# Loads and stores of a row gradient: from two DMA queues to one queue in strict turn

## The chip, the cores and the metric

The program runs on one core of a Trainium2 chip and uses no other. The metric is the device time of one execution in microseconds (us), given as the median over runs. Most runs of one kernel agree within 0.3%, so nothing below about half a per cent is read as an effect without several rounds on one chip.

## The reference

```python
def setup_inputs():
    return {"x": np.random.randn(8192, 8192).astype(np.float32)}

def reference(x):
    return np.gradient(x, axis=1)
```

Inside a row each output is half the difference of its two neighbours; at the two ends of a row it is the plain difference. Each element is read once and written once: 268.4 MB in and 268.4 MB out, 512 MiB in all.

## The kernel before

A tile holds two rows for each of the 128 partitions, 64 KB a partition, and there are 32 tiles and 3 buffers. VectorE writes the differences in place (the input sits 64 elements further on in the same buffer), ScalarE halves them. Loads are issued by SyncE on one DMA queue, stores by ScalarE on another.

```python
    R = 2
    SH = 64
    W = R * m
    pool = ctx.enter_context(tc.tile_pool(name="pool", bufs=3))

    # ... diff(b, c0, c1): tensor_sub on VectorE for the interior and for the
    # two end columns of a row, then nc.scalar.mul(..., mul=0.5) on ScalarE

        for i in range(nsets):
            last = i == nsets - 1
            b = pool.tile([P, SH + W], x.dtype)
            ls = m if last else W
            for c0 in range(0, W, ls):
                nc.sync.dma_start(                       # loads: queue of SyncE
                    out=b[:, SH + c0 : SH + c0 + ls],
                    in_=x_sets[i, :, c0 : c0 + ls],
                )
            step = m // 4 if last else m // 2
            for c0 in range(0, W, step):
                diff(b, c0, c0 + step)
                if last:
                    nc.scalar.dma_start(                 # the last tile leaves in 8 pieces
                        out=out_sets[i, :, c0 : c0 + step], in_=b[:, c0 : c0 + step]
                    )
            if not last:
                nc.scalar.dma_start(out=out_sets[i], in_=b[:, 0:W])   # stores: queue of ScalarE
```

Of the kernel before, what the change touches and what calls it, by code (L numbers as in the profile page):

```python
# [1 line left out]

# [4 lines left out]


@with_exitstack
def kernel(  # L10
    ctx: ExitStack,
    tc: tile.TileContext,
    x: bass.AP,
    out: bass.AP,
):





    nc = tc.nc
    P = nc.NUM_PARTITIONS
    n, m = x.shape
    R = 2
    SH = 64
    W = R * m
    nsets = n // (P * R)

    x_sets = x.rearrange("(s p t) m -> s p (t m)", p=P, t=R)
    out_sets = out.rearrange("(s p t) m -> s p (t m)", p=P, t=R)  # L30

    pool = ctx.enter_context(tc.tile_pool(name="pool", bufs=3))

    def diff(b, c0, c1):

        lo, hi = c0, c1
        if c0 % m == 0:
            lo = c0 + 1
            nc.vector.tensor_sub(  # L39
                out=b[:, c0:lo],  # L40
                in0=b[:, SH + c0 + 1 : SH + c0 + 2],
                in1=b[:, SH + c0 : SH + c0 + 1],
            )
        if c1 % m == 0:
            hi = c1 - 1
        nc.vector.tensor_sub(  # L46
            out=b[:, lo:hi],
            in0=b[:, SH + lo + 1 : SH + hi + 1],
            in1=b[:, SH + lo - 1 : SH + hi - 1],
        )  # L50
        if hi < c1:
            nc.vector.tensor_sub(  # L52
                out=b[:, hi:c1],
                in0=b[:, SH + hi : SH + c1],
                in1=b[:, SH + hi - 1 : SH + c1 - 1],
            )
        nc.scalar.mul(out=b[:, lo:hi], in_=b[:, lo:hi], mul=0.5)  # L57

    with tc.manual_schedule():
        for i in range(nsets):  # L60
            last = i == nsets - 1
            b = pool.tile([P, SH + W], x.dtype)

            ls = m if last else W
            for c0 in range(0, W, ls):
                nc.sync.dma_start(  # L66
                    out=b[:, SH + c0 : SH + c0 + ls],
                    in_=x_sets[i, :, c0 : c0 + ls],
                )
            step = m // 4 if last else m // 2  # L70
            for c0 in range(0, W, step):
                diff(b, c0, c0 + step)
                if last:
                    nc.scalar.dma_start(
                        out=out_sets[i, :, c0 : c0 + step], in_=b[:, c0 : c0 + step]
                    )
            if not last:
                nc.scalar.dma_start(out=out_sets[i], in_=b[:, 0:W])


# [1 line left out]
_INS = ['x']  # L82
_OUTS = [((8192, 8192), 'float32')]


# [23 lines left out]
```

## Time and profile before

1249.59 us was the median of three runs (1249.23 to 1252.78); the profiled run had a span of 1246.8 us.

| | before |
|---|---|
| share of the span that the two queues' packets fill, of 16 engines | 49.9% + 49.7% |
| VectorE busy, ScalarE busy | 47%, 37% |
| rate over the span | 431 GB/s |
| one 64 KB packet on one engine, median | 2.418 us |

The page of the profile shows the first three; the packet time is from the trace's packet records, which have the start, length, size and queue of every packet. The row "DMA" is the busy share of the 16 DMA engines in tenths in 40 slices of the span, the row "GB/s" what they moved; "q1" is SyncE's queue, "q10" ScalarE's, with packets, MB and share:

```profile
span 1246.8 us, 665 instructions
DVE 584.6 (47%) x260; ACT 464.9 (37%) x133; POOL 0.2 (0%) x4
...
DMA  9999999999999999999999999999999999999998
GB/s 404 437 435 437 427 421 433 437 437 435 438 435 437 437 435 416 429 437 437 437 433 437 437 435 437 435 414 433 437 437 435 435 438 435 437 435 433 426 426 343
DMA packets 10373, 536.92 MB, mean 431 GB/s; under 512 B 1152, under 2 KB 1152, under 8 KB 1152
...
q1 hardware_dynamic: 4752, 268.44, 49.9%
q10 hardware_dynamic: 5616, 268.44, 49.7%
```

Nine tenths in every slice but the last. The waits of the DMA issuer (who waited for whom, us in total, times, longest; L66 issues the loads):

```profile
SPq L66 <- DMA out_dram<-b: 1127.6, 29, 59.5
...
SPq L66 <- DMA b<-in_x_dram: 20.5, 1, 20.5
```

Loads waited 1,128 us, nine tenths of the span, for the stores that free their buffers. But what waits is the issuer. Whether it costs anything is seen in the engines, and in the middle of the run they had no hole (a hole is time in which none of the 16 engines has a data packet; view by windows: length, busy time of VectorE, ScalarE and GpSimd with counts, TensorE clock, DMA share, GB/s):

```profile
100.00:1150.00 1050.00, 489.59 (x215) 384.81 (x107) 0.00 (x0) 1.00 1.00 434
```

The last view needed is one tile's compute in the timeline, start and length first. The last ScalarE piece of tile 0 begins at 40.86 us, and the store is issued at 44.51, 22 us after the tile landed (22.56):

```profile
22.56 0.16 DVE L39 TENSOR_TENSOR b<-b 128x1 f32<-128x1 f32 x1 [22.56 <-DMA b<-in_x_dram]
...
40.86 3.62 ACT L57 ACTIVATE b<-b 128x4095 f32<-128x4095 f32 x1 [0.84 <-DVE b L46]
...
44.51 0.37 ACTq L78 DMA_DIRECT2D out_dram<-b  x1
```

### The profile page before, as it was taken

What the parts mean: (1) busy time and instruction counts of PE and PEld (TensorE: products, weight loads), DVE (VectorE), ACT (ScalarE), POOL (GpSimd) and SP (SyncE); (2) the same over time, 40 slices, a digit from 0 to 9 for tenths busy, and PEclk for the clock granted to TensorE, in tenths of its full rate; (3) what the DMA queues carried; (4) which work ended last, traced back from release to release, by engine and by line L of the source; (5) the groups of instructions that cost most, each with busy time, mean ns of one, the idle gap of its engine ahead of it and who ended that gap; (6) DMA issues with size and microseconds to landing.
All of it is one profiled execution on the core that took longest, in us unless ns stands there. A gap on an engine that the chain in (4) does not pass through costs nothing.

```text
span 1246.8 us, 665 instructions
## 1 busy us (share of the span) xinstructions
DVE 584.6 (47%) x260; ACT 464.9 (37%) x133; POOL 0.2 (0%) x4
## 2 busy tenths in 40 slices
DVE  2850555335553355533554335553355533555353
ACT  1731443234432344323442234432344323443252
POOL 0000000000000000000000000000000000000000
DMA  9999999999999999999999999999999999999998
GB/s 404 437 435 437 427 421 433 437 437 435 438 435 437 437 435 416 429 437 437 437 433 437 437 435 437 435 414 433 437 437 435 435 438 435 437 435 433 426 426 343
DMA packets 10373, 536.92 MB, mean 431 GB/s; under 512 B 1152, under 2 KB 1152, under 8 KB 1152
## 3 DMA queue, kind: packets, MB, share of 16 engines
q1 hardware_dynamic: 4752, 268.44, 49.9%
q10 hardware_dynamic: 5616, 268.44, 49.7%
q14 instruction: 5, 0.04, 0.0%
HBM read 268.44 MB, written 268.44 MB: 431 GB/s over the span
## 4 chain that ended last, share of the span: by engine, by line
DMA 75%; DVE 16%; another core or an unknown queue 4%; ACT 3%; issue 0%; SPq 0%; DVEq 0%
DMA b<-in_x_dram 38%; DMA out_dram<-b 37%; DVE b L46 16%; ACT b L57 3%; DVE b L39 0%; DVE b L52 0%; SPq L66 0%; DVEq L39 0%
## 5 line engine op out<-in xcount | busy, mean ns | idle before, releaser
L57 ACT ACTIVATE b<-b 128x4095 f32<-128x4095 f32 (+1 forms) x132 | 463.6, 3512 | 747.8 <-DVE b L46 747.8
L46 DVE TENSOR_TENSOR b<-b 128x4095 f32<-128x4095 f32 (+1 forms) x132 | 567.0, 4295 | 4.5
L39 DVE TENSOR_TENSOR b<-b 128x1 f32<-128x1 f32 x64 | 9.9, 155 | 642.3 <-DMA b<-in_x_dram 642.3
L52 DVE TENSOR_TENSOR b<-b 128x1 f32<-128x1 f32 x64 | 10.2, 159 | 2.2
L57 ACT ACT_TABLE_LOAD x1 | 1.3, 1283 | 22.6 <-DMA b<-in_x_dram 22.6
L93 POOL MEMSET const-bfloat16-1.0<- 128x1 bf16 x1 | 0.1, 101 | 0.0
L93 POOL MEMSET const-uint8-127<- 128x1 uint8 x1 | 0.1, 101 | 0.0
L93 POOL MEMSET const-float32-0.0<- 128x1 f32 x1 | 0.1, 98 | 0.2 <-issue 0.2
L93 POOL MEMSET const-float32-1.0<- 128x1 f32 x1 | 0.1, 98 | 0.0
## 6 DMA issues: line engine op xcount, KB each, us to landing
b<-in_x_dram SPq DMA_DIRECT2D x2, 4096.0 KB, 46.8
out_dram<-b ACTq DMA_DIRECT2D x8, 1024.0 KB, 18.7
b<-in_x_dram SPq DMA_DIRECT2D x31, 47.7
out_dram<-b ACTq DMA_DIRECT2D x31, 46.6
```

Source lines behind the costliest of these rows:

```text
L39: nc.vector.tensor_sub(out=b[:, c0:lo], in0=b[:, SH + c0 + 1 : SH + c0 + 2], in1=b[:, SH + c0 : SH + c0 + 1],)
L46: nc.vector.tensor_sub(out=b[:, lo:hi], in0=b[:, SH + lo + 1 : SH + hi + 1], in1=b[:, SH + lo - 1 : SH + hi - 1],)
L52: nc.vector.tensor_sub(out=b[:, hi:c1], in0=b[:, SH + hi : SH + c1], in1=b[:, SH + hi - 1 : SH + c1 - 1],)
L57: nc.scalar.mul(out=b[:, lo:hi], in_=b[:, lo:hi], mul=0.5)
L93: nc = _bacc.Bacc("TRN2", target_bir_lowering=False, num_devices=1)
```

## The change

The intent: with loads and stores on one queue, in strict turn, transfers no longer share the engines; each lands in half the time, and the order is chosen so that one transfer is always queued behind the running one. The load that reuses a buffer (`LAG = 3` buffers) is issued one turn late (`BACK = 1`), behind the next tile's store. So the queue reads load 0, load 1, load 2, store 0, store 1, load 3, store 2, load 4, and so on. The last tile is loaded whole and stored in two pieces.

```diff
-    pool = ctx.enter_context(tc.tile_pool(name="pool", bufs=3))
+    LAG, BACK = 3, 1
+    pool = ctx.enter_context(tc.tile_pool(name="pool", bufs=LAG))
...
+    def load(i):
+        b = pool.tile([P, SH + W], x.dtype)
+        nc.sync.dma_start(out=b[:, SH : SH + W], in_=x_sets[i])
+        return b
...
+        held = [load(i) for i in range(LAG)]
         for i in range(nsets):
-            ... (tile, load, diff, store on nc.scalar)
+            b = held[i]
+            piece = m if i == nsets - 1 else W
+            for c0 in range(0, W, m // 2):
+                diff(b, c0, c0 + m // 2)
+                c1 = c0 + m // 2
+                if c1 % piece == 0:
+                    nc.sync.dma_start(
+                        out=out_sets[i, :, c1 - piece : c1], in_=b[:, c1 - piece : c1]
+                    )
+            j = i - BACK
+            if j >= 0 and j + LAG < nsets:
+                held.append(load(j + LAG))
```

More of the change, by code (lines that the diff above doesn't have):

```diff
@@ L57, in diff @@
         nc.scalar.mul(out=b[:, lo:hi], in_=b[:, lo:hi], mul=0.5)
+    def load(i):
+        b = pool.tile([P, SH + W], x.dtype)
+        nc.sync.dma_start(out=b[:, SH : SH + W], in_=x_sets[i])
+        return b
     with tc.manual_schedule():
+        held = [load(i) for i in range(LAG)]
         for i in range(nsets):
-            last = i == nsets - 1
-            b = pool.tile([P, SH + W], x.dtype)
-            ls = m if last else W
-            for c0 in range(0, W, ls):
-                nc.sync.dma_start(
-                    out=b[:, SH + c0 : SH + c0 + ls],
-                    in_=x_sets[i, :, c0 : c0 + ls],
-                )
-            step = m // 4 if last else m // 2
-            for c0 in range(0, W, step):
-                diff(b, c0, c0 + step)
-                if last:
-                    nc.scalar.dma_start(
-                        out=out_sets[i, :, c0 : c0 + step], in_=b[:, c0 : c0 + step]
-                    )
-            if not last:
-                nc.scalar.dma_start(out=out_sets[i], in_=b[:, 0:W])
+            b = held[i]
[6 more added lines that the diff above has]
+                        out=out_sets[i, :, c1 - piece : c1], in_=b[:, c1 - piece : c1]
+                    )
+            j = i - BACK
+            if j >= 0 and j + LAG < nsets:
+                held.append(load(j + LAG))
 _INS = ['x']
```

## The prediction

> **What bounds it now.** The DMA engines, almost without a break. The page gives the two queues 49.9% + 49.7% of 16 engines' span, VectorE 47%, ScalarE 37%. In the trace's packet records a 64 KB packet takes 2.418 us at the median, load or store: 16 x 65,536 B / 2.418 us = 434 GB/s, against the ceiling of 435 GB/s in the Trainium skill, "DMA: Bandwidth & Descriptors", section "Where 436 GB/s comes from"; this trace agrees. 512 MiB is 512 such packets for each engine: 1238.0 us. The span is 1246.8 us, so under 9 us (0.7%) is anything else:
> - 1.7 us before the first packet of data,
> - 1.7 us of slow first packets (about 3.1 us each), 0.6 us of slow ones later,
> - 0.65 us of completion packets,
> - 0.4 us because the last tile is stored in 8 KB packets (309 ns; eight make 2.47 us),
> - some 3.5 us at the end: engines finishing unevenly, last receipt, last instructions.
>
> From 50 us to the tail, 16 data packets are in flight on average: the two queues leave no gap to fill. The 1,128 us that loads wait for stores (the waits of the DMA queue) are an issuer's waits; the engines are busy with the other queue.
>
> **What the change removes, adds, moves.** Same bytes, same 64 KB packets, same compute. Transfers take turns: each takes about 19.4 us instead of 47. Does the order keep the engines fed? Let load i land at t. Store i-1 runs to t+19.4, load i+1 to t+38.7. A tile's compute takes 22 us (22.56 to 44.51 in the timeline), so store i is queued at t+22, 16 us early; load i+2 waits for store i-1 (t+19.4 and a receipt), is queued just after, and is needed at t+58. At the start loads 0 to 2 run to about 61 us; store 0 is queued at 44.5. At the end store 30 covers most of the last tile's compute. Nothing of compute is exposed.
>
> **Does one queue hand over without a gap?** Loads 0 and 1 landed at about 22.5 and 41.9 us, with one queue running: 19.4 against 8 x 2.418 = 19.34. In the tail, after the last load, stores alone kept 16 packets in flight through four completions. So load to load and store to store cost below 0.1 us. A change of direction on one ring isn't shown by this trace; 63 at 0.1 us would be 6 us.
>
> **Predicted.** Gain: 0.4 us of small packets, perhaps 0.5 us of a tidier end. Loss: 0 to 6 us. I expect 1249.0 us, 8 in 10 between 1246 and 1255. Faster by over 2% would be 1225 us, below the 1238 us of packets. Chances: faster 0.005, same 0.965, slower 0.03.
>
> **What would show it.** One queue with 99% of the span, again 2.418 us a packet; DMA 9 tenths in every slice, some 430 GB/s; each transfer landing about 19.4 us after the one before; tiles computed every 38.7 us; VectorE and ScalarE as busy as before.
>
> **What would make it wrong.** A gap at each change of direction (0.4 us each makes 2%); packets slower when one direction runs alone for long; or load i+2 made to wait for a later store than i-1, which empties the queue for a receipt every turn, seen as deficits in DMA.

## The result and the profile after

| | before | after |
|---|---|---|
| median (range), runs | 1251.16 us (1249.23 to 1252.78), 4 | 1250.30 us (1249.71 to 1250.97), 4 |
| span of the profiled run | 1246.8 us | 1249.0 us |

The ratio is 0.9994, with a 95% interval of 0.9974 to 1.0014: the same.

The page after, with the same rows:

```profile
span 1249.0 us, 619 instructions
DVE 583.8 (47%) x256; ACT 464.1 (37%) x129; POOL 0.2 (0%) x4
...
DMA  9999999999999999999999999999999999999997
GB/s 403 437 432 420 428 432 432 437 434 437 434 424 435 432 434 430 432 437 432 437 434 434 437 434 434 430 428 432 434 428 435 437 430 434 432 437 437 437 437 332
...
q1 hardware_dynamic: 9360, 536.88, 99.6%
```

One queue has replaced two and fills the same 99.6%, and a 64 KB packet again takes 2.418 us at the median. The middle of the run, by windows, shows the same 1.00 share and the same 434 GB/s:

```profile
100.00:1150.00 1050.00, 491.87 (x215) 386.90 (x107) 0.00 (x0) 1.00 1.00 434
```

The waits of the issuer have changed completely (L77 issues stores, L63 loads). It waits for compute, since a tile's store comes next in its program. It hardly waits for stores any more, 34.5 us instead of 1,128:

```profile
SPq L77 <- DVE b L54: 1057.5, 32, 39.1
SPq L77 <- ACT b L59: 111.9, 33, 3.4
SPq L63 <- DMA out_dram<-b: 34.5, 2, 17.7
```

More than a thousand microseconds of waits went from one line to another and the time did not move. In the timeline of the issuer a turn is a store and, at once behind it, a load. Turns are 38.6 us apart, which is two transfers of 19.3 us:

```profile
417.22 0.33 SPq L77 DMA_DIRECT2D out_dram<-b  x1
417.60 0.42 SPq L63 DMA_DIRECT2D b<-in_x_dram  x1
455.81 0.33 SPq L77 DMA_DIRECT2D out_dram<-b  x1
456.20 0.42 SPq L63 DMA_DIRECT2D b<-in_x_dram  x1
```

### The profile page after: what moved, and what is told of

Same layout as the page of the kernel before. It is cut to its first block, busy times and chain, and to the rows that moved or that the text cites. A ratio compares the mean times of both kernels' runs of the same rounds, so it can differ in the third digit from the quotient of the medians.

```text
span 1249.0 us, 619 instructions
## 1 busy us (share of the span) xinstructions
DVE 583.8 (47%) x256; ACT 464.1 (37%) x129; POOL 0.2 (0%) x4
## 3 DMA queue, kind: packets, MB, share of 16 engines
q1 hardware_dynamic: 9360, 536.88, 99.6%
## 4 chain that ended last, share of the span: by engine, by line
another core or an unknown queue 45%; DVE 44%; DMA 8%; ACT 1%; issue 1%; DVEq 0%
DVE b L48 43%; DMA b<-in_x_dram 5%; DMA out_dram<-b 3%; DVE b L54 1%; DVE b L41 1%; ACT b L59 1%; DVEq L41 0%
## 5 line engine op out<-in xcount | busy, mean ns | idle before, releaser
L59 ACT ACTIVATE b<-b 128x4095 f32<-128x4095 f32 x128 | 462.8, 3616 | 744.7 <-DVE b L48 744.7
L48 DVE TENSOR_TENSOR b<-b 128x4095 f32<-128x4095 f32 x128 | 566.3, 4424 | 4.4
```

The source lines that it names most:

```text
L48: nc.vector.tensor_sub(out=b[:, lo:hi], in0=b[:, SH + lo + 1 : SH + hi + 1], in1=b[:, SH + lo - 1 : SH + hi - 1],)
L59: nc.scalar.mul(out=b[:, lo:hi], in_=b[:, lo:hi], mul=0.5)
```

## The experiments

Three readings of "same" had to be told apart. **A**: the 16 engines move 512 packets of 2.418 us each, from whatever queue, and both kernels keep them fed. **B**: strict turn gains something and the changes of direction on one ring cost as much. **D**: compute or its waits are on the path after all, and hide a gain. A further question was whether the queued transfer matters, as the change claims, or not (**C**). Each run below is of a kernel that differs from the changed one only as its diff shows, unless it says otherwise.

### Stores back on the second queue

```diff
-                    nc.sync.dma_start(
+                    nc.scalar.dma_start(
                         out=out_sets[i, :, c1 - piece : c1], in_=b[:, c1 - piece : c1]
```

> The changed kernel with its stores back on the second queue; order of program, buffers and the last pieces as changed. Theory A (the 16 engines move 512 packets of 2.418 us each whatever queue they come from): within 0.4% of both kernels, 1246 to 1255 us. Rival B (the one queue gains something by strict turn, and loses as much elsewhere): this one keeps the gain or the loss alone, so it differs from the changed kernel by over 0.5%.

Measured: 1248.39 us median of six (one outlier of 1266.4 keeps the interval wide), ratio to before 0.9992 (0.9945 to 1.0039). The median lies within 0.2% of the changed kernel's, which was measured in other rounds. As A expects; B's half a per cent isn't there by the medians, though the interval alone doesn't exclude it.

### No compute at all

```diff
-                diff(b, c0, c0 + m // 2)
...
-                        out=out_sets[...], in_=b[:, c1 - piece : c1]
+                        out=out_sets[...], in_=b[:, SH + c1 - piece : SH + c1]
```

> Wrong result on purpose: no compute at all, each tile is stored as it was loaded, same queue and order. Theory A: the transfers alone take all the time, so 1244 to 1251 us, within 0.4%. Rival D (something of the compute or its waits is on the path): faster by more than 0.5%.

Measured: 1249.66 us median of four, ratio to before 0.9976 (0.9944 to 1.0008); wrong result, as intended. Taking away 584 us of VectorE and 464 us of ScalarE moved the time by nothing that can be told from noise. D's half a per cent isn't there by the medians (0.2%), though the lower end of the interval, 0.9944, just reaches it. The page supports the medians: the one queue fills as much of a span of 1249.3 us as in the changed kernel, whose span was 1249.0 us. So D falls, as far as the noise lets one see: the transfers alone take all the time.

```profile
q1 hardware_dynamic: 9360, 536.88, 99.6%
```

### No transfer queued behind the store

```diff
-    LAG, BACK = 3, 1
+    LAG, BACK = 3, 0
```

> One queue, but the load that reuses a buffer is issued right after that buffer's store, so nothing is queued behind a store until it has landed. Theory A: a gap per tile of a receipt and an issue, estimated at 1.7 us (store 0 should end near 81.4 us and load 3 was issued at 82.0 in the changed kernel; a first packet starts about 1.0 us after its issue): 29 gaps, about 1300 us, 1275 to 1325, with the engines' busy share down by that much. Rival C (the queued transfer doesn't matter, the engines drift apart and hide the gap): within 1% of before.

Measured: 1354.98 us median of four, ratio 1.0818 (1.0776 to 1.0859). The direction was right and the size was twice what I expected: about 106 us more in the profiled span than the changed kernel's 1247 to 1249, over 29 turns 3.6 us each and not 1.7. The page shows the share of the one queue falling from 99.6% to

```profile
q1 hardware_dynamic: 9360, 536.88, 95.7%
```

and the windows show the middle of the run at 394 GB/s instead of 434:

```profile
100.00:1150.00 1050.00, 456.16 (x200) 361.58 (x100) 0.00 (x0) 1.00 0.96 394
```

The waits of the issuer are again loads waiting for stores, much as in the kernel before, and this time they cost 8%; theory C falls:

```profile
SPq L63 <- DMA out_dram<-b: 1203.8, 29, 42.1
SPq L77 <- DVE b L54: 74.1, 3, 39.1
```

The second line says why nothing was queued: it was not for want of a finished tile, as a store (L77) waited for compute only a few times. In the turn below, the store that is issued at 422.30 us is that of tile 9, computed by 382.2 us. In the program of SyncE it comes after the load that waits, and so it is issued only when that load has been.

The share shows 4 points of idle time, half of the loss. The other half hides in packets that take longer, which counts as busy. I followed one turn through the packet records (the engines' 64 KB packets in rounds of 16, one for each engine; all on one queue):

```
round starts (us)     packets took (us), shortest / median / longest
418.49 to 419.08      2.418  2.418  2.418    store, last packets; all done at 421.50
422.83 to 423.44      2.842  3.114  3.349    load, first packets
425.87 to 426.48      2.418  2.418  2.422
...
437.95 to 438.56      2.418  2.420  2.420
440.36 to 440.98      3.356  3.728  3.995    load, last packets
444.09 to 444.74      2.418  2.418  2.418    store, first packets
```

In the timeline the load was issued at 421.86, only 0.36 us after the last packet of the store, and the next store at once behind it:

```profile
421.86 0.33 SPq L63 DMA_DIRECT2D b<-in_x_dram  x1
422.30 0.37 SPq L77 DMA_DIRECT2D out_dram<-b  x1
```

Over the 29 turns an engine sat idle for 1.96 us on average (all 16 together for 1.32 us; there were exactly 29 such holes). The first packet of the load then took 0.66 us longer than 2.418, and the last packet of the load, before the engines turn to the store, 1.23 us longer. That makes 3.85 us, times 29 is 112 us: with the 1238.0 us of packets that leaves about 4 us of the span of 1353.9 us for start and end. My estimate of 1.7 us was of the idle part alone.

### Lookahead in the second half only

Why the last packet of a load is slow mattered for the prediction's open point, the change of direction. In the changed kernel the very first such packet, at the end of load 2, was 1.29 us too long too, and later ones much less. Two theories: **E**, it comes whenever all 16 engines turn from loads to stores at nearly the same time (in lockstep); **F**, it comes only at the first turn after a queue has been empty.

```diff
-            j = i - BACK
-            if j >= 0 and j + LAG < nsets:
+            back = 0 if i < nsets // 2 else 1
+            j = i - back
+            if j >= 0 and len(held) <= j + LAG < nsets:
                 held.append(load(j + LAG))
```

> The first 16 tiles in the order of no_lookahead (the queue runs empty once a tile), the rest in the order of the changed kernel. Loss: no_lookahead lost about 106 us in 29 turns, 3.6 us each, so half the turns should lose about 55 us: 1298 to 1312 us. What the packet records of the second half should tell: in no_lookahead the last packet of every load, the one before the engines turn to a store, took 1.1 to 1.5 us longer than 2.418 us. Theory E (lockstep: all 16 engines turn at once): the second half starts in lockstep too, so its first few loads end with packets 1 us or more longer. Theory F (it comes once after a queue has run empty): from the second load after the last empty queue on, below 0.4 us.

Measured: 1310.57 us median of four, ratio 1.0459 (1.0413 to 1.0505). The records have 16 holes, the last ending at 720.0 us, and none after. I put the packets in order for each engine and counted eight to a transfer. Around the change of order, as means over the 16 engines, the loads look like this:

```
transfer  starts (us)  spread of starts   idle before  first packet   last packet
32 load   677.8        1.23 us            2.08 us      +0.60 us       +1.29 us
34 load   720.2        0.76 us            1.91 us      +0.65 us       +1.18 us
37 load   780.0        0.76 us            0.00 us      +0.06 us       +0.23 us
39 load   819.0        1.52 us            0.00 us      +0.00 us       +0.21 us
41 load   857.8        2.14 us            0.00 us      +0.00 us       +0.14 us
```

Loads 34 and 37 start equally close together (0.76 us between the first engine and the last), and only the one behind a hole pays. E expected 1 us or more for load 37; it was 0.23. E falls as the main cause, F stands, by the packet records of this one profile. What the engines do during the 1.2 us is not in the records and stays open.

### Engines put out of step before the first turn

```diff
-        held = [load(i) for i in range(LAG)]
+        held = [load(0)] + [room() for i in range(1, LAG)]      # room(): a buffer, no load
+        p0, c = 0, 2048
+        for k in range(15, 0, -1):
+            nc.sync.dma_start(
+                out=held[2][p0 : p0 + k, SH : SH + c], in_=x_sets[2, p0 : p0 + k, 0:c]
+            )
+            p0 += k
+        for i in range(1, LAG):
+            nc.sync.dma_start(out=held[i][:, SH : SH + W], in_=x_sets[i])
```

> The changed kernel with 15 small extra loads behind load 0 (of 15, 14, ... 1 partitions, 8 KB each, into a buffer that load 2 overwrites), to put the engines out of step by up to 4.5 us before the first turn from load to store; result still correct. Theory E (lockstep): the last packet of load 2, 1.2 to 1.3 us too long in the changed kernel, is less than 0.5 us too long on average. Theory F (first turn after an empty queue): still 0.8 us or more. The time: 1250 to 1258 us, as the engine with the most extra packets ends some 4.5 us later than else, less what drifting would have cost anyway. If the small loads should go to the engines in another way than a ramp, the spread of starts in the packet records will say so, and then nothing follows.

Measured: 1257.91 us median of four, ratio 1.0034 (0.9998 to 1.007). The experiment failed in its design. The issuer had to wait for some of its small loads, and engines ran dry:

```profile
SPq L76 <- DMA b<-in_x_dram: 21.3, 8, 19.1
```

By the packet records the engines started the rest of load 1 within 0.7 us of each other again, so there was no ramp, and nothing follows about E or F. In the profiled run an engine sat idle for 3.0 us on average in this stretch. The time, 1257.91 us beside a median of 1252.23 us for the kernel before in the same rounds, is not clear of noise.

### Twice the turns, and twice the transfers with the same turns

The first has tiles of one row and six buffers, 128 transfers in strict turn:

```diff
-    R = 2
-    LAG, BACK = 3, 1
+    R = 1
+    LAG, BACK = 6, 1
```

> Tiles of one row and six buffers: twice the transfers (128 of 4 MB, packets of 32 KB) and twice the changes of direction on the one queue. To be read against two_pieces, which has the same 128 transfers but half the changes. Theory A (a change of direction costs under 0.1 us): the two are within 6 us (0.5%) of each other, both 1246 to 1260 us. Rival B (a change costs 0.2 us or more, made up for elsewhere in the changed kernel): this one is 13 us or more above two_pieces.

The second keeps the tiles and issues each load and each store as two transfers of one row:

```diff
-        nc.sync.dma_start(out=b[:, SH : SH + W], in_=x_sets[i])
+        for c in range(0, W, m):
+            nc.sync.dma_start(
+                out=b[:, SH + c : SH + c + m], in_=x_sets[i, :, c : c + m]
+            )
...
-                if c1 % piece == 0:
-                    nc.sync.dma_start(out=out_sets[i, :, c1 - piece : c1], ...)
+                if c1 == W:
+                    for c in range(0, W, m):
+                        nc.sync.dma_start(out=out_sets[i, :, c : c + m], ...)
```

> The changed kernel with each load and each store issued as two transfers of one row each (32 KB packets), so 128 transfers with as many changes of direction as in the changed kernel. Theory A: 1246 to 1258 us; the difference to the changed kernel is the cost of 64 more hand-overs and of smaller packets, under 0.5%. Rival B: as the changed kernel, and below one_row by 13 us or more.

Beside both, the changed kernel once more:

> The changed kernel again, timed on the same chip as one_row and two_pieces, to have all three side by side: 1248 to 1252 us, ratio to before between 0.997 and 1.003.

| | median of six | ratio to before (95%) |
|---|---|---|
| changed kernel again | 1249.20 us | 0.9983 (0.9968 to 0.9998) |
| one row, 128 transfers, twice the turns | 1251.00 us | 0.9995 (0.9981 to 1.0010) |
| two pieces, 128 transfers, same turns | 1254.55 us | 1.0023 (1.0006 to 1.0039) |

B wanted the kernel with twice the turns to be at least 13 us slower than the one with the same number of transfers; it was 3.6 us faster. Against the changed kernel it has 63 more transfers and 58 more changes of direction (117 for 59) and is 1.8 us slower, so that one more of both costs about 0.03 us as long as something is queued. B falls. Why two pieces are the slowest of the three is open; the profiles show only where the time is: the engines ended their last packets between 1243.1 and 1251.9 us of the span, in the changed kernel between 1241.0 and 1246.2 us.

### The kernel before with two buffers

```diff
-    pool = ctx.enter_context(tc.tile_pool(name="pool", bufs=3))
+    pool = ctx.enter_context(tc.tile_pool(name="pool", bufs=2))
```

> The kernel before with two buffers in place of three. Theory A: buffers matter only as far as they keep work queued. Two buffers on two queues: worked through with 19.4 us a transfer, 22 us of compute and 1.7 us of receipt, two tiles take about 80 us instead of 77.4, with gaps while both tiles compute: 1270 to 1310 us. Rival: the third buffer is spare and this is within 1% of before.

Measured: 1366.30 us median of four, ratio 1.0895 (1.085 to 1.094), worse than the 1270 to 1310 us that I expected, and far from the rival's 1%. The two queues together had

```profile
q1 hardware_dynamic: 4752, 268.44, 48.1%
q10 hardware_dynamic: 5616, 268.44, 46.8%
```

of the span. The packet records show 27 holes of 1.4 to 4 us in which no engine had a data packet, 49.8 us together, one every 42 us in most of the run; packets restarted slowly after them, as above. I had counted the idle time but not the slow restart, and had the pattern of the turns wrong. So with two queues it is the third buffer that keeps work queued. One queue with two buffers was not run.

## Why the prediction was right

The time was predicted as 1249.0 us with a range of 1246 to 1255 and 96.5% for "within 2%"; it was 1250.3 us, ratio 0.9994.

- *The engines are the bound, with 1238.0 us of packets.* Right, and shown by the run without compute: 1249.66 us.
- *The order keeps one transfer queued, and nothing of compute is exposed.* Right: no hole in the packet records of the changed kernel, share 1.00 from 100 to 1150 us, turns of 38.6 us. The store issued at 417.22 us was reached by the engines at 430.6 us on average, 13 us later; I had said 16, not counting that the engines drift apart and a load lands with its last engine. At the very end a little compute did show: in the profile after, the first half of the last store was issued at 1222.37 us, and eight engines that were done with store 30 sat idle for 0.6 to 1.5 us. It made the end no later, since the slowest engine was busy with store 30 until 1228.5 us. The run without lookahead shows what the order is worth: 8.2%.
- *The 1,128 us of loads waiting for stores are an issuer's waits.* Right: 34.5 us were left after, and the time stayed.
- *Load to store on one ring isn't shown; 0.1 us each would be 6 us.* The right size for turns that no hole precedes: the last packet of a load before a store was on average 0.07 us too long over the 29 such turns of each profiled run of the changed kernel (0.071 and 0.065 us, at most 0.31), 2 us together. That it fitted was in part luck: 0.1 us was a guess, as the prediction says itself. It was wrong as a general picture: the first turn after an empty queue cost about 1.2 us (1.23 on average over the 29 of the run without lookahead). And the trace of the kernel before held more on this than the prediction saw. There each engine, from 49 us on, mostly took a load packet and a store packet in turn from its two queues, at 2.419 us each on average, so a change of direction as such cost next to nothing. Only the 16 load packets just before the first stores, begun at 45.9 to 46.4 us, were 1.02 us too long. The prediction seems to have counted these among its 1.7 us of "slow first packets": the very first packets make up only 0.7 us of it. So the slow first turn is not a matter of the single queue.
- *A gain of 0.4 us of small packets and 0.5 us of a tidier end.* Not to be seen. The last packets of the fastest and the slowest engine were 5.2 us apart in the profile after (1242.7 and 1247.9 us), as in the one before (1240.4 and 1245.6 us). The repeat measured 0.9983 (0.9968 to 0.9998), the first measurement 0.9994; I make nothing of either.

No kernel tried here beats both by more than the noise, and at this packet rate none with these bytes can by much: 1238.0 us of the 1247 or so of span are full-rate packets.

## What to carry to other kernels

In this kernel, whose packets fill 99% of the span at their full rate, queues, turns and issuers' waits were ways of arriving at the same time: in such a case, compute bytes over the measured packet rate first, and look for a gap in the engines, not in the issuer. If everything goes through one queue, issue the transfer that must wait for a store one turn late, behind something that is ready. Otherwise the ready transfer stands behind the waiting one in the issuer's program, and the queue runs empty (here 8%, with 1,204 us of waits that look just like the harmless 1,128 us of the two-queue kernel). The busy share understated such a hole here, as half of its cost was slow packets after it.

## What the Trainium skill lacked or had wrong

- "DMA: Bandwidth & Descriptors", section "Issuing engines are not separate DMA queues", says that issuing from several engines only saves the sequencer's issue time. That holds here for bandwidth (1248.39, 1249.20 and 1251.44 us, with two, one and two queues), but the section leaves out that a wait on one issuing engine holds up the ready transfers behind it in its program, which a second issuing engine with its own queue is free of: without lookahead two queues lose nothing (the kernel before) and one queue loses 8.2%. No run gives one issuer two queues, so issuer and queue are not told apart.
- The same page, section "Anatomy of one DMA — SWDGE (gpsimd) path", gives a fixed cost of about 2.0 us a DMA for the software path. The queues here are not on that path (the page of the profile lists them as hardware_dynamic), so no run here tests the figure; the idle part of a hole, 1.96 us an engine, was of the same size. No page has the slow packets that follow, 0.66 us more on the first and 1.23 us more on the last packet of the load, which make a hole cost 3.85 us.
- "SBUF — State Buffer", section "Summary: rules for kernel authors", tells to estimate transfers between HBM and SBUF with about 358 GB/s. By that page's figure an estimate for these 512 MiB is 1,500 us; this program, on one core, moved 431 GB/s over the span and 434 in the middle, reads and writes together. "HBM Reference", section "Specifications (TRN2)", says that a core alone is bounded by its DMA engines, and this agrees: their packets fill 99.6% of the span.
